# One-core kernel, sum of squared differences: the wait for the last store and the clearing of semaphores go from GpSimd to SP

## Chip, cores, metric

The kernel runs on one core of a Trainium2 chip. The metric is the device time of an execution in microseconds (us). The profile's span, from the first to the last instruction of the program, is shorter than this time. TensorE has no work and the granted clock was 1.000.

## The reference

```python
# x, y: 1024 x 4096 float32, axis = -1
def reference(x, y, axis):
    return np.sum((x - y) ** 2, axis=axis).astype(np.float32)
```

The two inputs are 33.55 MB together; the output is 4 KB.

## The kernel before

All loads and the one store are issued by SP. VectorE subtracts, ScalarE squares with a sum along the row, and VectorE adds the partial sums of the rows that were cut. Semaphores are allocated by hand through a small helper, and have to be back at zero when the program ends. The parts that the change touches:

```python
class Program:
    # ...
    def close(self, sem, value):
        self.nc.gpsimd.wait_ge(sem, value)
        self.nc.clear_and_free_semaphores(self.sems)     # GpSimd: DRAIN, then one range clear

def tile_sub_square_sum_kernel(tc, x, y, axis, out):
    # ... [cut: layout, sizes of the loads]
    prog = Program(nc, tc)
    diffs = prog.semaphore("diffs")
    acts = prog.semaphore("acts")
    sums = prog.semaphore("sums")
    stored = prog.semaphore("stored")
    # ... [cut: one semaphore per load, the loads, subtraction, squares, sums of parts]
    complete(7)                                            # the last reduction, on VectorE

    nc.sync.wait_ge(sums, n["sums"])
    nc.sync.dma_start(out=ov, in_=results).then_inc(stored, 16)
    prog.close(stored, 16)
```

So at the end SP waits for the sums and issues the store, GpSimd waits for the store's 16 increments, and then GpSimd clears all 19 semaphores in one instruction, a range clear. The DRAIN ahead of it is an instruction of GpSimd's sequencer.

## Time and profile before

| | before |
|---|---|
| time, median of the first 3 runs | 85.19 us (85.11 to 85.19) |
| the profiled run | 85.35 us, span 83.5 us |
| end of the last arithmetic (VectorE's reduction) | 81.79 us |
| last increment of the store's semaphore | 83.23 us |
| end of GpSimd's range clear, the end of the span | 83.51 us |
| last mark of the runtime's second barrier | 85.47 us |

The last four rows are counted from the start of the span. The increments and the marks are from the trace's record of semaphore updates, which goes on after the program's last instruction; the page doesn't print it. The section of the page on idle time shows no wait of GpSimd for the store, because that wait is one of the sequencer (POOLq) and not of the engine.

### The profile page before, as it was taken

Reading aid. Unit: us, or ns where it says so; the run is one execution under the profiler, and the core shown is the slowest. Engines: PE = TensorE matmul, PEld = TensorE weight load, DVE = VectorE, ACT = ScalarE, POOL = GpSimd, SP = SyncE. Lnnn points to the kernel's source line nnn. Section 1 sums busy time; section 2 is a strip of 40 time slices with the busy share of each in tenths; the row PEclk is TensorE's granted clock in tenths of the full one; section 3 lists DMA queues with packets and bytes.
Section 4 is the critical chain, followed back from the end, with each engine's and each line's share of the span. In section 5 each row is a group of like instructions: output and inputs, shape, how many; then the busy total and the mean of one; then the engine's idle time right before and its main releaser. Section 6 shows DMA issues by size and latency. Waiting matters only on the chain.

```text
span 83.5 us, 109 instructions
## 1 busy us (share of the span) xinstructions
DVE 36.3 (44%) x18; ACT 31.7 (38%) x27; POOL 0.2 (0%) x4
## 2 busy tenths in 40 slices
DVE  0000000000000000000299999999099995979980
ACT  0500000000000000000001979697970897989990
POOL 0000000000000000000000000000000000000000
DMA  9389999956999999589989998997999899999920
GB/s 471 157 377 502 502 502 502 471 251 283 497 497 497 497 497 404 218 373 497 439 377 439 487 439 345 487 487 330 423 437 437 378 443 427 423 407 410 394 66 2
DMA packets 2305, 33.56 MB, mean 402 GB/s; under 512 B 385, under 2 KB 769, under 8 KB 1409
## 3 DMA queue, kind: packets, MB, share of 16 engines
q1 hardware_dynamic: 2304, 33.56, 94.7%
q14 instruction: 1, 0.00, 0.0%
HBM read 33.55 MB, written 0.00 MB: 402 GB/s over the span
## 4 chain that ended last, share of the span: by engine, by line
DMA 68%; ACT 14%; DVE 14%; SPq 1%; issue 0%
DMA Y<-in_y_dram 68%; ACT X L171 14%; DVE X L165 14%; SPq L108 1%; DVE results L178 0%; SPq L215 0%
## 5 line engine op out<-in xcount | busy, mean ns | idle before, releaser
L165 DVE TENSOR_TENSOR X<-X,Y 128x4096 f32<-128x4096 f32 (+9 forms) x14 | 35.8, 2593 | 45.2 <-DMA Y<-in_y_dram 45.1
L171 ACT ACTIVATE X<-X 128x4096 f32<-128x4096 f32 (+8 forms) x13 | 29.7, 2287 | 48.0 <-DVE X L165 48.0
L171 ACT ACTIVATION_READ_ACCUMULATOR X<-X 128x1 f32 x13 | 2.4, 186 | 0.0
L171 ACT ACT_TABLE_LOAD x1 | 1.3, 1283 | 1.9 <-PEq L19 1.9
L178 DVE TENSOR_REDUCE results<-parts 128x1 f32<-128x2 f32 (+1 forms) x2 | 0.3, 152 | 0.2 <-ACT X L171 0.2
L199 DVE CUSTOM_DVE_ANT_0 Y<-X,parts 128x160 f32<-128x160 f32 x1 | 0.4, 385 | 0.0
L244 POOL MEMSET const-bfloat16-1.0<- 128x1 bf16 x1 | 0.1, 101 | 0.0
L244 POOL MEMSET const-uint8-127<- 128x1 uint8 x1 | 0.1, 101 | 0.0
L244 POOL MEMSET const-float32-0.0<- 128x1 f32 x1 | 0.1, 98 | 0.2 <-issue 0.2
L244 POOL MEMSET const-float32-1.0<- 128x1 f32 x1 | 0.1, 98 | 0.0
L199 DVE DVE_READ_ACCUMULATOR2_ANT results<- 128x1 f32 x1 | 0.1, 83 | 0.0
## 6 DMA issues: line engine op xcount, KB each, us to landing
Y<-in_y_dram SPq DMA_DIRECT2D x1, 8112.0 KB, 40.7
X<-in_x_dram SPq DMA_DIRECT2D x1, 4096.0 KB, 48.9
Y<-in_y_dram SPq DMA_DIRECT2D x1, 4096.0 KB, 58.3
X<-in_x_dram SPq DMA_DIRECT2D x1, 2784.0 KB, 13.4
Y<-in_y_dram SPq DMA_DIRECT2D x1, 1456.0 KB, 19.2
Y<-in_y_dram SPq DMA_DIRECT2D x1, 1328.0 KB, 16.2
X<-in_x_dram SPq DMA_DIRECT2D x1, 912.0 KB, 21.0
Y<-in_y_dram SPq DMA_DIRECT2D x1, 464.0 KB, 21.6
```

Source lines behind the costliest of these rows:

```text
L108: nc.sync.dma_start(out=dst[:, home(c0, c1)], in_=src[:, c0:c1]).then_inc(sem, 16)
L165: nc.vector.tensor_sub(out=a, in0=a, in1=Y[:, home(c0, c1)]).then_inc(diffs, 1)
L171: nc.scalar.activation(out=a, in_=a, func=Square, accum_out=acc).then_inc(acts, 1)
L178: nc.vector.tensor_reduce(out=results[:, r : r + 1], in_=parts_of(r, len(row_parts[r])), axis=mybir.AxisListType.X, op=add,).then_inc(sums, 1)
L199: nc.vector.tensor_tensor_reduce(out=Y[:, home(*piece)], in0=X[:, home(*piece)], in1=X[:, home(*piece)], scale=1.0, scalar=parts_of(r, 1), ...
L244: nc = _bacc.Bacc("TRN2", target_bir_lowering=False, num_devices=1)
```

## The change

The intent is to take the clear off the path to the end: SP clears all semaphores but the store's own while the store is under way, then waits for the store and takes its 16 away in the same instruction. GpSimd is not used at the end any more. The rest of the diff only rewrites the program's Python.

```diff
-    def close(self, sem, value):
-        self.nc.gpsimd.wait_ge(sem, value)
-        self.nc.clear_and_free_semaphores(self.sems)
+    def close(self, engine, stored, value):
+        engine.sem_clear(range(self.sems[0].num, self.sems[-1].num + 1))
+        engine.wait_ge(stored, value).then_inc(stored, -value)
@@
     prog = Program(nc, tc)
+    stored = nc.alloc_semaphore("stored")
     diffs = prog.semaphore("diffs")
     acts = prog.semaphore("acts")
     sums = prog.semaphore("sums")
-    stored = prog.semaphore("stored")
@@ [cut: the splitting of a load into rows becomes a helper, pieces_of, used twice]
         if j == 4:
-            complete(6)
+            for r in (6,):
+                complete(r)
     complete(7)

     nc.sync.wait_ge(sums, n["sums"])
     nc.sync.dma_start(out=ov, in_=results).then_inc(stored, 16)
-    prog.close(stored, 16)
+    prog.close(nc.sync, stored, 16)
```

More of the change, by code (lines that the diff above doesn't have):

```diff
@@ L127, with pieces_of @@
     row_parts = [[] for _ in range(R)]
-    for c0, c1 in ys:
+    def pieces_of(c0, c1):
+        pieces = []
         while c0 < c1:
             e = min(c1, (c0 // D + 1) * D)
-            row_parts[c0 // D].append((c0, e))
+            pieces.append((c0, e))
             c0 = e
+        return pieces
+    for c0, c1 in ys:
+        for piece in pieces_of(c0, c1):
+            row_parts[piece[0] // D].append(piece)
     parts, where = None, {}
@@ L188 @@
         wait_loaded(c1, landed_y[j][1])
-        pieces = []
-        while c0 < c1:
-            e = min(c1, (c0 // D + 1) * D)
-            pieces.append((c0, e))
-            c0 = e
-        for piece in pieces:
+        for piece in pieces_of(c0, c1):
             sub(*piece)
```

## The prediction

> **What bounds the kernel now.** I read the page from the top, then the chain that ended last, then the last 6 us of the timeline, and last the queue records of GpSimd, because the change touches nothing before the end. The page's ledger and the slices by time:
>
> ```profile
> span 83.5 us, 109 instructions
> ...
> DVE 36.3 (44%) x18; ACT 31.7 (38%) x27; POOL 0.2 (0%) x4
> ...
> DMA  9389999956999999589989998997999899999920
> ...
> HBM read 33.55 MB, written 0.00 MB: 402 GB/s over the span
> ```
>
> The reader is to see that the kernel is a stream of 33.55 MB: the DMA row is at 9 in most slices, VectorE and ScalarE are busy for less than half of the span, and only the last two of the 40 slices (2.1 us each) hold no transfer to speak of. The chain says the same with a short tail:
>
> ```profile
> 54.11 16.24 DMA Y<-in_y_dram
> 70.35 0.02 issue
> 70.37 2.94 DVE X L165
> 73.31 0.02 issue
> 73.33 8.28 ACT X L171 x14
> 81.61 0.02 issue
> 81.64 0.16 DVE results L178
> ```
>
> The columns are start, length, and what ran. Arithmetic ends at 81.64 + 0.16 = 81.80 us, while the span is 83.5 us. So 1.7 us lie behind the last arithmetic, and the chain does not name what fills them, because it leaves out semaphore work. The timeline and the records of lines 226 and 46 name it:
>
> ```profile
> 81.64 0.16 DVE L178 TENSOR_REDUCE results<-parts 128x1 f32<-128x5 f32 x1 [0.23 <-ACT X L171]
> 81.82 0.35 SPq L226 DMA_DIRECT2D out_dram<-results  x1
> ```
>
> ```profile
> out_dram<-results SPq DMA_DIRECT2D x1, 4.0 KB, 1.4
> ```
>
> ```profile
> L46 POOLq DRAIN  x1: 88/88/88, 83.3 to 83.3; - x1
> L46 POOLq EVENT_SEMAPHORE_RANGE_CLEAR  x1: 138/138/138, 83.4 to 83.4; - x1
> ```
>
> The store is issued on SP from 81.82 to 82.17 us (0.35) and lands 1.4 us after its start; the trace's single records of its semaphore lie between 83.07 and 83.23 us. GpSimd, which waits for that, starts its DRAIN at 83.26 (88 ns, to 83.35), and its range clear at 83.37 (138 ns, to 83.51). The clear is the last instruction of the program: it **is** the end of the span. So in this tail the store's flight, about 1.06 us from the end of its issue to its last increment, has nothing beside it, and 0.28 us of GpSimd's work follows it.
>
> A time of 85.19 us against a span of 83.5 us says that 1.7 us more are counted outside the span (the profiled run itself took 85.35, so 1.84 there). The trace keeps the semaphore updates of that part too. Semaphore 2, which no instruction of the kernel names, gets nine increments in one round: the first already at 2.13 us, the second at 81.72, the third only at 84.04, then 84.08, 84.11, 84.20, 84.24, 84.28 and 84.32. From 84.24 to 84.89 some 200 semaphores are set in runs, and a second round of nine goes from 85.12 to 85.47. That is a barrier of the five engines after the program, a reset, and another barrier. I read the order of the engines from their last instructions: the first to come is TensorE, which has no work; the second is ScalarE (its last read of the accumulator ended at 81.60); the third is the one that everything then waited for, GpSimd, 0.53 us after its clear ended. VectorE and SP, done since 81.79 and 82.17, follow 45 and 23 ns later. This barrier is what the change shortens, more than the span.
>
> **What the Trainium skill says.** "Runtime: NRT & Kernel Launch", section "The ~15µs preamble/postamble breakdown", lists a barrier after the kernel, then a reset of 51 semaphores per engine, then a barrier again, and describes the barrier as a serpentine over five engines at 44 ns a hop and 8 hops. The trace agrees in kind: nine increments, and in the undisturbed round ahead of the program they take 371 ns, 46 ns a hop. It does not agree in size for the reset, which the page puts at about 1.5 us: here its writes take 0.65 us. "Perfetto Trace Analysis", section "Sequencer-only Instruction (DRAIN, etc)", says that the reported window leaves out the wait before and the propagation after. Here it fits: 24 ns lie between the last increment of the store and the start of GpSimd's DRAIN, in no record. "DMA: Bandwidth & Descriptors", section "Anatomy of one DMA — SWDGE (gpsimd) path", explains for the GpSimd path that a transfer's fixed cost of about 2 us is mostly the receipt of the last byte; this store of 4 KB is issued by SP, but the trace has 1.4 us[...], and the change cannot shorten it, only use it.
>
> **The change part by part.** The streams of the compiled kernels differ in three things only; loads, arithmetic and the store are the same in number, shape and order, as the helper for the pieces and the loop over one row only rewrite the program's own Python.
>
> 1. Removed from GpSimd: the wait, its DRAIN and its range clear. From the store's last increment (83.23) to the end of the clear (83.51) that is 24 + 88 + 29 + 138 = 279 ns, all on the path to the end.
> 2. Added to SP, right behind the store's issue: the same range clear. SP is free at 82.17. Consecutive issues on SP stand about 50 ns apart in this trace (the first ends 0.377 us after its start, the second starts at 0.427), so the clear runs from about 82.22 to 82.36 if it takes GpSimd's 138 ns. The store lands at 83.23, so 0.87 us of slack remain; even four times as long it would be hidden.
> 3. Added to SP: one instruction that waits for the store and subtracts 16. The same form, a wait with a subtraction, stands in the barriers ahead of the program, at 17 ns. With GpSimd's 24 ns of waking it ends at 83.23 + 0.02 + 0.02 = 83.27. So the **span** becomes 83.27, or 0.24 us less.
> 4. Moved: who comes last to the barrier. Before, GpSimd came 0.53 us after its last instruction, and SP, the fifth, 68 ns after that, at 84.11. Now GpSimd is ready from the start, and SP is last. When does SP come? The trace has three such distances from last instruction to increment: ScalarE 0.12 us, TensorE 0.24[...], GpSimd 0.53. [...]I choose 0.2 us: it comes at 83.47, and the fifth increment moves from 84.11 to 83.47, by 0.64 us. What follows (return of the barrier, reset, second barrier) I take as unchanged. With ScalarE's distance the gain is 0.72, with GpSimd's 0.31.
>
> Sum: 85.19 - 0.64 = 84.55; leaning a little to the smaller gain because SP's distance is nowhere in this trace, 0.59 us and **84.60 us**, 0.7% less.
>
> **The rivals.** First, that the gain is only what the span shows: if the 0.53 us between the clear and the barrier belong to whatever engine ends last and not to GpSimd, SP pays them too. For it: nothing in this trace shows SP's own. Against: two of three engines are much quicker. Time then 85.19 - 0.31 = 84.88. Second, that the wait for the store takes the place of everything: the end is the store's latency and the clear was hidden or outside the measured time. Against: the clear starts 0.14 us after the last increment and the barrier visibly waits for it. Time then 85.1 to 85.2. Third, that the clear delays SP, so that it and not the store becomes the bound: it would have to take over 1 us against 138 ns, and the time would rise by the excess. Fourth, that the stream moves: the loads are DMA-bound, and the semaphores' numbers and the code's length shift slightly; I know no reason in the profile for more than the spread of the three runs, 0.08 us.
>
> **Range and chances.** The low end is the ScalarE-like distance with 0.17 us for spread between runs and rounds: 84.30. The high end is the first rival with 0.07 for spread: 84.95. Two per cent are 1.70 us; the whole part between the store's landing and the third increment is 0.81 us (83.23 to 84.04), so a faster verdict would need something that I do not see: 0.02. Slower by 2% needs a stall or a disturbed stream: 0.01. Within 2%: 0.97.
>
> **What would show it.** In the changed profile the range clear should stand on SP near 82.2 us, the wait with its subtraction at about 83.26 for some 17 ns, and no GpSimd record after the first 2 us; the span should read 83.3. The gap between span and time should shrink too, by 0.2 to 0.5 us; if it does not, the first rival holds. A clear that starts late or lasts past 83.2 would prove the third. A last load that lands more than 0.2 us earlier or later than now would mean that the difference came from the stream, and that my account of the end was not what was measured.

## The result, and the profile after

The changed kernel takes 84.42 us (median of 4 runs, 84.32 to 84.52); the kernel before took 85.16 us in the same rounds (85.11 to 85.19). The ratio is 0.9914, with a 95% interval of 0.9897 to 0.9931: 0.74 us less. Ratios are the mean time of one kernel's fast runs over that of the other's fast runs of the same rounds, so not quite the ratio of the medians quoted.

The page of the changed kernel, the same lines as were shown of before:

```profile
span 83.0 us, 109 instructions
...
DVE 36.3 (44%) x18; ACT 31.7 (38%) x27; POOL 0.2 (0%) x4
...
DMA  9299999929999997599799979979999999999940
...
HBM read 33.55 MB, written 0.00 MB: 404 GB/s over the span
```

The work is the same, and so is the number of instructions: a DRAIN and a clear on GpSimd have gone, a clear and a wait on SP have come. The chain, in order of time (start, length, what):

```profile
0.43 40.44 DMA Y<-in_y_dram
...
53.87 16.23 DMA Y<-in_y_dram
70.09 0.02 issue
70.12 2.94 DVE X L170
73.05 0.02 issue
73.07 8.29 ACT X L176 x14
81.37 0.02 issue
81.39 0.16 DVE results L183
```

The last reduction starts at 81.39, not 81.64. The reader is to see that these 0.25 us were there already at the first long load, which took 40.44 us here; in the profile of before the same line of the chain reads "0.43 40.69 DMA Y<-in_y_dram". Everything between that landing and the reduction has the same lengths. That is the stream's own spread: over all profiles the line lay between 40.38 and 40.79 us, and in rewrite_only below, which has before's end, it is 40.45. So the spans of two single profiles must not be subtracted; their ends have to be compared from a common event, and I use the landing of the store. The end of the timeline, and the two instructions of the new end:

```profile
81.39 0.16 DVE L183 TENSOR_REDUCE results<-parts 128x1 f32<-128x5 f32 x1 [0.25 <-ACT X L176]
81.58 0.35 SPq L227 DMA_DIRECT2D out_dram<-results  x1
```

```profile
L44 SPq EVENT_SEMAPHORE_RANGE_CLEAR  x1: 62/62/62, 82.0 to 82.0; - x1
```

```profile
L45 SPq EVENT_SEMAPHORE  x1: 17/17/17, 83.0 to 83.0; - x1
```

The three numbers with slashes are the shortest, median and longest duration in ns. The clear runs on SP from 81.97 to 82.04 us, 0.96 us before the store's last increment at 82.995; the wait starts 17 ns after that and ends the span at 83.03. GpSimd has nothing to do after its preparations.

Semaphore 2 counts the runtime's barrier. I call each of its increments a mark and the time from one mark to the next a hop. Nine marks make a round: in the first five the engines report one after the other, the other four are the way back. From the records of semaphore updates, with the landing (the store's sixteenth increment) as zero:

| us after the landing | before | after |
|---|---|---|
| last instruction of the program ends | 0.279 (GpSimd) | 0.034 (SP) |
| that engine's mark in the runtime's barrier | 0.806 (third) | 0.176 (fifth) |
| SP's mark, the fifth | 0.874 | 0.176 |
| next mark, the first on the way back | 0.971 | 0.219 |
| last mark of the second barrier | 2.239 | 1.487 |

The last row differs by 0.752 us, which is the whole of the measured 0.74. The part up to the program's last instruction is 0.245 of it. The distance from an engine's last instruction to its mark, which I call the engine's tail, went from 0.527 (GpSimd) to 0.142 (SP): 0.385. As SP is the fifth, the two hops from third to fifth (0.068) are gone from the path, and the first hop back is 0.043 and not 0.097 (0.054). 0.245 + 0.385 + 0.068 + 0.054 = 0.752.

### The profile page after: what moved, and what is told of

Same layout as the page of the kernel before. It is cut to its first block, busy times and chain, and to the rows that moved or that the text cites. A ratio compares the mean times of both kernels' runs of the same rounds, so it can differ in the third digit from the quotient of the medians.

```text
span 83.0 us, 109 instructions
## 1 busy us (share of the span) xinstructions
DVE 36.3 (44%) x18; ACT 31.7 (38%) x27; POOL 0.2 (0%) x4
## 4 chain that ended last, share of the span: by engine, by line
DMA 68%; ACT 14%; DVE 14%; SPq 1%; issue 0%
DMA Y<-in_y_dram 68%; ACT X L176 14%; DVE X L170 14%; SPq L107 1%; DVE results L183 0%; SPq L215 0%
```

## The experiments

Theory: the gain is where this table puts it, and most of it is a matter of **which engine ends last**: GpSimd's tail is long and its place in the barrier is not the last. Rivals: the tail belongs to a range clear (or to the DRAIN) as last instruction, on any engine; it is a matter of where the code lies; the stream of loads was moved by the rewriting; clears aren't really hidden under the store. Twelve runs were made, one of them of the changed kernel again, all with correct results, in three lots, each on another chip; the kernel before had medians of 85.16, 85.24 and 85.23 us in the three. "Landing to end" is the last row of the table above, "tail" as above, both from each run's profile.

| run | who ends, with what | median us | ratio to before | landing to end | tail |
|---|---|---|---|---|---|
| before | GpSimd, DRAIN and clear | 85.16 | 1 | 2.239 | 0.527 |
| change | SP, wait | 84.42 | 0.9914 | 1.487 | 0.142 |
| change_again | SP, wait | 84.56 | 0.9913 | 1.484 | 0.142 |
| rewrite_only | GpSimd, DRAIN and clear | 85.11 | 0.9990 | 2.236 | 0.527 |
| pool_late | GpSimd, clear | 85.07 | 0.9987 | 2.119 | 0.527 |
| pool_wait | GpSimd, wait | 84.90 | 0.9966 | 2.034 | 0.562 |
| sp_late | SP, clear | 84.45 | 0.9913 | 1.514 | 0.125 |
| act_wait | ScalarE, wait | 84.70 | 0.9934 | 1.654 | 0.150 |
| dve_wait | VectorE, wait | 84.75 | 0.9945 | 1.624 | 0.188 |
| sp_single | SP, wait after 18 clears | 84.50 | 0.9914 | 1.522 | 0.139 |
| sp_36 | SP, wait after 36 clears | 85.50 | 1.0029 | 2.532 | 0.139 |
| sp_overrun | SP, wait after 54 clears | 87.25 | 1.0236 | 4.188 | 0.647 |
| sp_pad | SP, wait; 54 clears earlier | 84.55 | 0.9913 | 1.521 | 0.179 |
| pool_pad | GpSimd, wait; 54 clears earlier | 85.28 | 1.0005 | 2.036 | 0.567 |

The intervals of the ratios are about 0.002 to either side, 0.17 us, so differences below that are read from the traces alone, and count as seen in one profile each. The part after the program's last instruction can be checked in every run, as time minus span (spans are listed to 0.1 us). It is 1.79 to 1.91 us in all runs in which GpSimd ends, 1.28 to 1.41 where SP does (sp_overrun apart), 1.47 to 1.53 with ScalarE and 1.41 to 1.47 with VectorE.

### rewrite_only: the rewritten text with the old end

```diff
-    def close(self, engine, stored, value):
-        engine.sem_clear(range(self.sems[0].num, self.sems[-1].num + 1))
-        engine.wait_ge(stored, value).then_inc(stored, -value)
+    def close(self, sem, value):
+        self.nc.gpsimd.wait_ge(sem, value)
+        self.nc.clear_and_free_semaphores(self.sems)
```

(with the store's semaphore back in the program's list)

> The changed kernel's text with the old end put back: GpSimd waits for the store and clears all semaphores. Theory (the whole gain of 0.74 us comes from the end): no gain, 85.16 us within 0.1, the range clear on GpSimd about 0.28 us after the store's last increment and GpSimd's mark in the barrier about 0.53 us after the clear. Rival (the rewritten Python or the moved semaphore number shifted the stream, which ended 0.25 us earlier in the profile after): about 84.9 us.

Measured: 85.11 us, ratio 0.9990 (0.9969 to 1.0012); the lines of GpSimd's two instructions:

```profile
L46 POOLq DRAIN  x1: 88/88/88, 83.1 to 83.1; - x1
L46 POOLq EVENT_SEMAPHORE_RANGE_CLEAR  x1: 138/138/138, 83.2 to 83.2; - x1
```

They have before's durations, and the landing to the end takes 2.236 us. In this profile the first long load took 40.45 us, as in the profile of the change, and yet there is no gain. The rewriting makes no difference that these runs show, and the early landing in the profile of the change was not the source of its gain.

### sp_late: SP, in the old order

```diff
-        engine.sem_clear(range(self.sems[0].num, self.sems[-1].num + 1))
-        engine.wait_ge(stored, value).then_inc(stored, -value)
+        engine.wait_ge(stored, value)
+        engine.sem_clear(range(stored.num, self.sems[-1].num + 1))
```

> SP does everything, but in the old order: it waits for the store and clears afterwards. Theory (the engine that ends last sets the tail; the clear itself is only 62 ns on SP): the clear with its gap returns to the path, 0.06 to 0.11 us, so about 84.50 us, and SP's mark in the barrier comes about 0.14 us after the clear. Rival (the 0.53 us tail of before belongs to a range clear that is the last instruction, on whatever engine): a further 0.39 us, about 84.9 us.

Measured: 84.45 us, ratio 0.9913, which the times cannot tell from the change. The wait was merged into the clear, so that one instruction ends the program:

```profile
L45 SPq EVENT_SEMAPHORE_RANGE_CLEAR  x1: 64/64/64, 83.0 to 83.0; - x1
```

It takes 64 ns in place of the wait's 17, and the tail after it was 0.125 and not 0.142, so landing to end grew by 0.027 us only, less than either theory had. The rival is refuted: a range clear as last instruction has no tail of 0.53 us on SP. And the part of the change that its description names first, the clear under the store, is worth 0.03 us once the clear is on SP.

### pool_late and pool_wait: GpSimd, without the DRAIN, and with nothing but the wait

pool_late:

```diff
-        engine.sem_clear(range(self.sems[0].num, self.sems[-1].num + 1))
-        engine.wait_ge(stored, value).then_inc(stored, -value)
+        self.nc.gpsimd.wait_ge(stored, value)
+        self.nc.gpsimd.sem_clear(range(stored.num, self.sems[-1].num + 1))
```

> GpSimd waits and then clears, as before, but the wait is a plain one and the DRAIN of 88 ns is gone. Theory (the tail is GpSimd's): only the DRAIN is saved, some 0.09 us, about 85.07 us, and the mark still comes about 0.5 us after the clear. Rival (the DRAIN causes the tail): about 84.65 us.

pool_wait:

```diff
         engine.sem_clear(range(self.sems[0].num, self.sems[-1].num + 1))
-        engine.wait_ge(stored, value).then_inc(stored, -value)
+        self.nc.gpsimd.wait_ge(stored, value).then_inc(stored, -value)
```

> SP clears under the store as in the change, but GpSimd does the last wait with its subtraction, without DRAIN and without clear. Theory (GpSimd's own tail of 0.53 us against SP's 0.14, and its place in the barrier, third and not fifth): 0.39 + 0.07 + 0.05 = 0.51 us lost against the change, about 84.93 us. Rival (the tail came from the clear or the DRAIN): GpSimd's mark 0.14 us after its wait, about 84.54 us.

Measured: 85.07 and 84.90 us. First the last instruction of pool_late, then that of pool_wait:

```profile
L45 POOLq EVENT_SEMAPHORE_RANGE_CLEAR  x1: 138/138/138, 83.0 to 83.0; - x1
```

```profile
L45 POOLq EVENT_SEMAPHORE  x1: 17/17/17, 83.0 to 83.0; - x1
```

GpSimd's mark comes 0.527 us after the clear without a DRAIN ahead of it, and 0.562 us after a wait of 17 ns with neither clear nor DRAIN. So neither is what makes the tail; GpSimd as the last engine is. What GpSimd does in that time is in no record, so why its tail is the longest stays open. The three steps from before to the change can now be put beside each other on the scale of landing to end: DRAIN dropped, 2.239 to 2.119 (0.120); clear moved under the store on SP, to 2.034 (0.085); last wait moved from GpSimd to SP, to 1.487 (**0.547**). The times show the last step too: a median of 84.90 against 84.42 us, and the intervals of the two ratios are apart.

### act_wait and dve_wait: other engines wait last

```diff
-        engine.wait_ge(stored, value).then_inc(stored, -value)
+        self.nc.scalar.wait_ge(stored, value).then_inc(stored, -value)   # dve_wait: self.nc.vector
```

> SP clears under the store, ScalarE does the last wait with its subtraction. Theory (tail of the engine plus its place in the barrier): ScalarE's tail 0.115 us is shorter than SP's 0.14, but it is second in the barrier, so 0.106 us of hops to the fifth follow, and the first hop back is 0.097 and not 0.043: from landing to the end of the second barrier 1.62 us against 1.487, so about 84.55 us. Rival (only the tail counts): 84.40 us. In the trace: the third, fourth and fifth marks within 0.11 us after the second.

> SP clears under the store, VectorE does the last wait with its subtraction. Theory: tail 0.15 us as VectorE showed after its reduction, fourth in the barrier, one hop of 0.023 to SP, first hop back 0.097: from landing to the end 1.57 us, so about 84.50 us. Rival (the place doesn't matter): 84.43 us. Only the trace tells these apart with certainty.

The last instruction of act_wait, then that of dve_wait:

```profile
L45 ACTq EVENT_SEMAPHORE  x1: 17/17/17, 83.4 to 83.4; - x1
```

```profile
L45 DVEq EVENT_SEMAPHORE  x1: 21/21/21, 83.1 to 83.1; - x1
```

Measured: 84.70 and 84.75 us, ratios 0.9934 (0.9916 to 0.9953) and 0.9945 (0.9924 to 0.9966). In act_wait the second mark is the late one, at 0.188 us after the landing, and the third, fourth and fifth follow at 0.226, 0.270 and 0.293. In dve_wait the fourth is late, at 0.237, and the fifth follows at 0.260. That shows the order of the engines in the barrier, which the prediction only inferred: ScalarE second, GpSimd third (late in before), VectorE fourth, SP fifth. The tails were longer than I had taken (0.150 and 0.188); these engines now end with a wait and not with work, but whether that is the reason is not shown. Landing to end became 1.654 and 1.624 where 1.62 and 1.57 were expected. ScalarE's tail is within 0.01 us of SP's, but its run ends 0.167 us later: 0.105 of it in the hops to the fifth mark and 0.055 in the first hop back (0.097 or 0.098 where another engine came late, 0.043 or 0.044 where SP did). The place counts. In the times both runs are slower than the change by more than the traces say (0.2 to 0.3 us), but with overlapping intervals. The surplus lies ahead of the end: time minus span is 1.49 and 1.44 us on average against 1.32 in the change, 0.17 and 0.12 more, and the traces have 0.16 and 0.12 for that part.

### sp_single, sp_36, sp_overrun: how much is free under the store

```diff
-        engine.sem_clear(range(self.sems[0].num, self.sems[-1].num + 1))
+        for s in self.sems:                # sp_36: self.sems * 2, sp_overrun: self.sems * 3
+            engine.sem_clear(s)
         engine.wait_ge(stored, value).then_inc(stored, -value)
```

> The change with one clear for each of the 18 semaphores in place of one range clear, all behind the store's issue on SP. Theory (what SP does under the store is free while it takes under 1.0 us): 18 times some 0.05 us = 0.9 us, just within, so 84.42 us and an unchanged distance from landing to end of 1.49 us. Rival (clears delay the store or its landing): later by the time that they take, up to 85.3 us.

> The same with three times as many clears, 54. Theory: 54 times some 0.05 us = 2.7 us, which runs over the 1.0 us of the store's flight by 1.7 us, so about 86.1 us (the cost of one clear is taken from the run with 18); the store lands when it did. Rival (clears take no time worth naming, so nothing was ever hidden): 84.42 us.

> 36 single clears behind the store in place of 54. One clear with its gap took 57 ns, so they end some 2.1 us after the issue of the store, 1.0 us after it has landed; the wait then passes at once. If the tail is short (0.14 us): 84.42 + 1.04 = about 85.5 us; if it is long (0.65 us): about 86.0 us. Theory A leaves open which, B says long.

Measured: 84.50, 87.25 and 85.50 us. The clears of sp_36 and sp_overrun, then the last wait of sp_overrun:

```profile
L45 SPq EVENT_SEMAPHORE_RANGE_CLEAR  x36: 25/28/35, 82.2 to 84.2; - x36
```

```profile
L45 SPq EVENT_SEMAPHORE_RANGE_CLEAR  x54: 25/30/44, 82.7 to 85.8; - x54
```

```profile
L46 SPq EVENT_SEMAPHORE  x1: 17/17/17, 85.9 to 85.9; - x1
```

A single clear takes 28 to 30 ns in the median and the next starts 58 to 59 ns after it on average. Eighteen last from 82.14 to 83.17 us and just fill the flight of the store: it landed at 83.15, the wait started 0.058 us after that and not 0.017, and the time is the change's within the interval. With 36 the wait started 1.068 us after the landing, so 1.05 us more than in the change, and landing to end grew by 1.045. In all three the store landed 1.44 us after the last reduction, in the change 1.45. So the clears did not delay it. In these runs, then, clears on SP are free until the store has landed and cost their full time beyond.

The 86.1 us for sp_overrun were missed by 1.15 us. 0.5 of that are the clears, 59 ns each and not 50: the wait started 2.214 us after the landing where I had 1.7. Another 0.5 are a tail of 0.647 us on SP, which none of my theories had; the remaining 0.1 is of the size by which the kernel before differs between the lots.

### sp_pad, pool_pad, change_again: is the tail a matter of the code's length?

```diff
+    pad = nc.alloc_semaphore("pad")
     stored = nc.alloc_semaphore("stored")
@@ after the first four loads
+    for _ in range(54):
+        nc.sync.sem_clear(pad)             # pool_pad: nc.gpsimd, on top of pool_wait
```

> The changed kernel, unedited, in the same rounds as the next three. All theories: 84.42 us within 0.1, SP's mark 0.14 us after its wait.

> The change with 54 idle clears of an unused semaphore on SP in the middle of the loads, where SP has some 50 us to spare; the end has the one range clear and the wait. In the run with 54 clears at the end SP's mark came 0.65 us after its wait and not 0.14. Theory A (a longer stream of SP's instructions moves what follows it, so the tail depends on the length of the code): tail 0.65 us, about 84.9 us. Theory B (54 clears on end leave SP no pause before the runtime's own instructions): tail 0.14 us, 84.42 us.

> The run in which GpSimd does the last wait, with 54 idle clears on GpSimd at its beginning, while the loads run. If GpSimd's tail of 0.56 us is its own at any length of code: 84.90 us as without them, mark 0.56 us after the wait. If it is a matter of where its code lies: another tail, by some tenths of a us.

Measured: 84.56, 84.55 and 85.28 us; change_again lies 0.14 above 84.42, more than expected, but so does the kernel before in that lot by 0.07, and the ratio is the same, 0.9913. In sp_pad SP's tail was 0.179 us: the length of SP's code alone does not make 0.647. sp_36 had shown 0.139 after 36 clears without a pause, so a lack of a pause alone, with 36 clears, doesn't make it either. The two together, longer code and no pause, were not taken apart. It was seen only with 54 clears right before the end, in all six runs of it (time minus span 1.79 to 1.85 us, against 1.30 to 1.36 in sp_36). The cause stays open. In both runs with 54 clears on SP the trace has a fetch of instructions of 8 KB that the change's doesn't have, at 83.3 us in sp_pad and at 86.98 in sp_overrun; the latter starts after the mark it would have to explain.

In pool_pad GpSimd's tail was 0.567 us and landing to end 2.036, as in pool_wait: 54 more instructions do not move it. The time missed its expectation by 0.38 us, all ahead of the end. The chain of pool_wait, then of pool_pad, first long load:

```profile
0.42 40.39 DMA Y<-in_y_dram
```

```profile
0.41 40.79 DMA Y<-in_y_dram
```

Time minus span is 1.87 us on average, 1.88 in pool_wait. This load was the longest of its line in all profiles. In its lot change_again too had 40.65 us, so part may be the lot; whether GpSimd's clears, from 1.9 to 5.6 us, added the rest was not tested.

## Why the prediction was right

The time, 84.42 us, is within the range of 84.30 to 84.95, and no verdict of 2% either way was the likely one. That it lies there doesn't prove the middle of it: SP's distance to the barrier was in no trace, the 0.2 us for it was a choice between 0.12 and 0.53, and the range holds both ends. So the direction and the mechanism were foreseen, and the closeness of the number owes something to luck. Step by step:

1. Removed from GpSimd: 279 ns between landing and end of the span, replaced by 34 ns on SP. The prediction had 17 ns and 24 for waking; the trace has 17 and 17. Right.
2. The clear on SP: expected at about 0.05 us after the issue's end and for 138 ns; it came 50 ns after it and took 62. The slack of 0.87 us was 0.96. The duration was taken from the wrong engine, without consequence, as it was hidden.
3. The span: 83.3 us was expected and 83.0 found. 0.25 us of the difference to before is the first long load, which has no part in the change; from the landing the span's end moved by 0.245, where 0.24 was expected. The spans of the change's four runs are 83.0 to 83.2.
4. The barrier: the main step, and the one with a choice in it. SP's tail was taken as 0.2 us and was 0.142, so it gave 0.06 more. What follows SP's mark was taken as unchanged; the first hop back became shorter by 0.054. And the leaning to the smaller gain took 0.05 from the sum. 0.59 + 0.06 + 0.054 + 0.05 = 0.754, the 0.752 of the table within rounding. So the mechanism was right and its size too small by a fifth.
5. First rival (SP pays GpSimd's tail): refuted by the profile after, and pool_wait and sp_late show that the tail goes with the engine. Time minus span was to shrink by 0.2 to 0.5 us; it went from 1.84 to 1.32 on average in the runs listed, just beyond that. Second rival (nothing but the store's latency): refuted. Third (the clear delays SP): not with one clear, and sp_36 shows what it would look like. Fourth (the stream moves): it does vary by up to 0.4 us from profile to profile, but rewrite_only shows no gain from it.
6. A sign of being wrong came true: a last load landing more than 0.2 us earlier or later was to mean that the stream made the difference. It landed at 80.20 us and not at 80.47, 0.27 earlier. The sign was drawn too tightly for single profiles (80.15 to 80.93 over all of them), and two runs answer it: in rewrite_only the last load landed at 80.28 with no gain, in change_again at 80.41, almost as in before, with the same ratio as the change.
7. Two readings were loose, without consequence for the sum: the chain does hold semaphore work (SP's wait on line 215), it only isn't followed back from the end of it; and the last slice but one still moved 66 GB/s.

The change's stated idea, to hide the clear under the store, gave the smaller part. Nothing that was run beats the changed kernel. What wasn't tried is leaving out the wait for the store: its increments might then fall among the resets after the program, and a run might begin with a semaphore that is not zero; no run here shows it.

## What to carry to other kernels

Here the measured time followed the barrier after the program, which waited for the last engine, and not the last arithmetic; so look at who does the last instruction and compare time with span, not only at the chain of work: here 0.55 us of 85 (in the traces; 0.48 in the medians) hung on a wait of 17 ns standing on GpSimd and not on SP. Of the four engines tried, SP, which also issued the store, was the best place for the last wait; a store issued by another engine was not tried. Put what must still be cleared behind the issue of the store, where it was free for as long as the store flew (1.07 us here). Compare two profiles from a common event near the change: here two spans differed by 0.25 us that arose before the end.

## What the Trainium skill lacked or had wrong

- "Runtime: NRT & Kernel Launch", section "The ~15µs preamble/postamble breakdown", gives about 1.5 us for the barrier after the kernel and about 1.5 us for the reset of semaphores. Here, before, the barrier takes 0.285 us from the last engine's mark to its end (84.04 to 84.32), and 0.81 us from the program's last instruction (0.30 in the change); the writes of the reset take 0.65 us (84.24 to 84.89). Its 44 ns a hop are close (23 to 49 ns), but the hop at SP, the turning point, took, in the first round after the program, 97 to 98 ns where another engine came late and 43 or 44 where SP did.
- The same section doesn't say how long an engine takes from its last instruction to that barrier, nor in which order engines come. Here it is 0.53 to 0.57 us on GpSimd, 0.13 to 0.18 on SP (0.65 in one case that stays open), 0.15 on ScalarE and 0.19 on VectorE, in the order ScalarE, GpSimd, VectorE, SP after the first mark.
- No page that I found has the cost of a clear of semaphores by the kernel itself. Here a range of 18 or 19 takes 138 ns on GpSimd and 57 to 66 ns on SP; clears one after the other stand 58 to 59 ns apart on SP and 71 ns on GpSimd.
- "DMA: Bandwidth & Descriptors", section "Anatomy of one DMA — SWDGE (gpsimd) path", has about 2 us of fixed cost per transfer. It says so of GpSimd's path, so it is not contradicted, but that section has no figure for a transfer issued by SP. The store of 4 KB issued by SP took 1.41 to 1.42 us from the start of its issue to its last increment.
